# Attention logits from 64-row products, the heads in turn on the two halves of the TensorE array

## The chip, the cores and the metric

The kernel runs on one core of one Trainium2 chip. The metric is the device time of one execution in microseconds (us), the median of several runs. A second, profiled execution gives the trace from which the views below are taken; its time is given beside its span.

## The reference

One decoder layer over 2048 rows of width 1024, in fp32. What matters here are the two kinds of attention logits, both with heads of 64 channels:

```python
h = rms_norm(x, pre_norm_g[layer])
proj = h @ w_in[layer]
a_u, a_v, sq, sk, sv, mq, z = jnp.split(proj, split_at, axis=-1)
...
# window attention: 4 query heads, 2 key heads (g = 2 queries per key head), blocks of 128 rows
logits = jnp.einsum('bnqhgd,bnjhd->bnhgqj', qb, kb).astype(jnp.float32) * (dh ** -0.5)
...
# cross-attention: 4 heads into 256 memory tokens
logits = jnp.einsum('bshd,bmhd->bhsm', q, mem_k).astype(jnp.float32) * (dh ** -0.5)
...
y = jnp.concatenate([y_a, y_b, y_c], axis=-1) * jax.nn.silu(z)
x = x + rms_norm(y @ w_out[layer], post_norm_g[layer])
```

## The kernel before

Every fp32 operand of a product is held as two fp32r pieces, a rounded one (called the high piece) and the remainder (the low piece). An ordinary product takes three passes over the array: high by high, high by low, low by high. `split` makes the two pieces: a ScalarE (ACT) cast for the high one, a VectorE (DVE) subtraction for the low one.

The rows are worked on in four stretches t = 0 to 3 of 512 rows. In each, the order on TensorE is written out by hand: the v projection (line 1152), then the projections sv, k, q (two), mq (two) and z (four) in `group` (line 452), in odd stretches also the product for u and z of two stretches together (line 896, `set_a`). A last phase multiplies by w_out (line 1476). Between every six matmuls of 512 columns stands a `slot()`; tables of numbers at the head of the file say at which slot of which stretch a step is issued: loads, splits, the three stages of each attention unit (`A_STARTS`, `A_TURN`, `A_END`). TensorE and SyncE (SP, which issues the loads and stores) keep the order of the code; a scheduler orders the other engines.

An attention unit has three stages: logits and softmax, transposition of the probabilities, product with the values. A window unit (lines 622 to 680) does one block of 128 rows for all four heads, so there are 4 units in each stretch. A memory unit (lines 684 to 725) does one head for 256 rows, so there are 8 in each stretch, and the unit numbers 4 to 11 go through head 0's two halves (`cc` 0 and 1), then head 1's, and so on.

Heads have 64 channels and the array has 128 rows, and the kernel before uses that so: `split_heads` (line 601) writes one head's high piece of the queries to partitions 0 to 63 and its low piece to partitions 64 to 127, from one half of the projected rows at a time, so it takes two ACT and two DVE instructions of 64 partitions for a projection. The keys are written twice, to the upper and to the lower 64 partitions (the second time by an ACT copy, line 1202; for the memory keys line 579). One matmul of 128 rows then gives (high + low) queries by the high keys, a second the same by the low keys: two passes for each head instead of three. Each logits tile `lg` fills one PSUM bank of the pool `ps_t`, which has four; transposed probabilities, value products and others take their banks from the same pool. The transposed pieces `pT` have one buffer in SBUF.

The lines that the prediction speaks of: 641 (window logits), 691 (memory logits), 502 (a small product with 33 rows and 4 columns, `bv`), 605 and 606 (the query splits), 1202 (the second copy of the keys), 708 (transposes of the memory unit), 153 (the low piece in `split`), 250 (a weight unit loaded back from DRAM).

Of the kernel before, what the change touches and what calls it, by code (L numbers as in the profile page):

```python
# [33 lines left out]
STORE_AFTER = 6  # L34
# [3 lines left out]
TURN_SLOT = 26  # L38
# [10 lines left out]
LOADS = ((18, 25, 15, 29, 31), (66, 67, 66, 64, 68), (8, 10, 18, 19, 24, 23, 28, 31))  # L49
MAKES = ((29, 30, 30, 32, 33, 29, 42, 36),  # L50
         (70, 66, 67, 73, 76, 76, 90, 88),
         (16, 16, 21, 22, 24, 25, 34, 33))
A_STARTS = ((10, 16, 18, 26, 35, 38, 41, 41, 47, 50, 56, 58),
# [3 lines left out]
A_TURN = ((7, 10, 11, 8, 11, 8, 5, 8, 10, 9, 11, 9),  # L57
# [3 lines left out]
A_END = ((14, 14, 15, 14, 18, 10, 18, 14, 10, 13, 9, 12),  # L61
# [11 lines left out]
MIX_SLOTS = ((53, 56, 58),  # L73
             (49, 59, 61),
             (58, 61, 62),
             (62, 63, 67),
             (62, 68, 70),
             (67, 67, 73),
             (68, 72, 75),
             (73, 77, 79))  # L80
# [3 lines left out]
WO_SLOTS = ((4, 13, 13, 15, 17, 21), (35, 41, 49, 51, 58, 57))  # L84
WO_LOADS = ((-1, 3, 2, 17), (31, 29, 33, 55))
T_SLOTS = (-24, -12, -9, 4)
T_TILES = (1, 1, 1, 1)
T_STEPS = ((0, 3, 6, 6, 7), (3, 10, 10, 12, 12), (3, 5, 9, 11, 12), (2, 4, 7, 9, 9))
H_SUMS = (((-18, -14, -13, -15, -9, -7, -13, -7, -7, -6, -4),
# [7 lines left out]
H_SPARE = ((-7, 7), (20, 21))  # L97
H_LOADS = (((28, 26, 35, 39), (40, 43, 47, 42), (47, 48, 47, 54)),
           ((31, 35, 36, 32), (31, 40, 38, 41), (50, 51, 43, 57)))
H_OPS = (((35, 38, 36, 42), (52, 54, 54, 53), (49, 54, 50, 61)),  # L100
         ((37, 40, 42, 42), (50, 48, 53, 55), (52, 52, 56, 59)))
H_STORE = (3, 1)
Y_SUMS = ((-17, -11, -7), (-7, -2, -1))
Y_OPS = ((64, 71, 65, 77, 71), (71, 82, 83, 82, 82))
Y_WEIGHTS = (63, 81)
VALUES = (9, -2, 6, 6)
PUT_OFF = (5, 0, 0, 8, 6, 4)
# [3 lines left out]
def kernel(  # L111
# [227 lines left out]
    def first_stats():  # L339

        ss = tiny.tile([P, 4], F32, tag="ss", name="ss_0")
        for i in range(4):
            if i % 2 == 0:
                xp = sp.tile([P, 2, D], F32, tag="pT", name=f"xp_{i}", bufs=1)
# [72 lines left out]
    def load_x(t, ks, tag):  # L417
# [5 lines left out]
        if tag == "s4b":  # L423
            a = new_spare(1, raw=True).rearrange("p s (k n) -> p (s k) n", k=2)
        else:
            a = sp.tile([P, len(ks), TS], F32, tag=tag, name=f"xj_{t}_{ks[0]}", bufs=1)
# [46 lines left out]
    bias_0 = cp.tile([P, 4, P], F32, name="bias_0")  # L473
# [39 lines left out]
    def bias_turned():  # L513

        for i in range(2):
# [7 lines left out]
    MK = cp.tile([P, 4, 2, MEM], F32R, name="MK")  # L523
# [34 lines left out]
    def project_memory(u):  # L558
# [12 lines left out]
        if u < 2:  # L571
# [26 lines left out]
    carry = cp.tile([P, 2, 2, P], F32R, name="carry")  # L598
    SV = cp.tile([P, 5, 2, 2, 64], F32R, name="SV")

    def split_heads(ps, tag, shape_tag):
        S = sp.tile([P, 2, TS], F32R, tag=shape_tag, name=f"S_{tag}", bufs=1)
        for e in range(2):
            src = ps[64 * e : 64 * e + 64, :]
            nc.scalar.copy(S[0:64, e, :], src)  # L605
            nc.vector.tensor_tensor(S[64:128, e, :], src, f32(S[0:64, e, :]), ALU.subtract)
# [15 lines left out]
    def window_unit(t, c, S, O, done):  # L622
# [13 lines left out]
        for kv in range(2):  # L636
            hs = slice(2 * kv, 2 * kv + 2)
            lg = ps_t.tile([P, 2, 256], F32, tag="t", name=f"l_{tag}_{kv}")
            for e in range(2):
                for s in range(2):  # L640
                    nc.tensor.matmul(lg[:, e, :], S[kv][:, e, c * P : (c + 1) * P],
                                     keys[t][:, kv, s, c * P : c * P + 256], start=(s == 0), stop=(s == 1))
            if first:
                nc.vector.scalar_tensor_tensor(Lc[:, hs, :P], lg[:, :, P:], scale, bias_0[:, hs, :], ALU.mult, ALU.add)
                continue
# [11 lines left out]
        both = sp.tile([P, 2, 2, 4, P], F32R, tag="pT", name=f"pT_{tag}", bufs=1)  # L657
# [24 lines left out]
    pTs = {}  # L682

    def memory_unit(t, h, cc, S, O, done):

        tag = f"c{t}_{h}_{cc}"
        lg = ps_t.tile([P, 2, 256], F32, tag="t", name=f"l_{tag}")
        for e in range(2):
            q0 = (2 * cc + e) * P
            for s in range(2):  # L690
                nc.tensor.matmul(lg[:, e, :], S[:, h % 2, q0 : q0 + P], MK[:, h, s, :],
                                 start=(s == 0), stop=(s == 1))
# [16 lines left out]
        if cc == 0:  # L709

            pTs[h] = sp.tile([P, 2, 2, 2, 256], F32R, tag="pT", name=f"pT_{tag}", bufs=1)
# [110 lines left out]
    def first_sums():  # L822

        def some(k, s):
            r = {}

            def load():
                if k:
                    both = sp.tile([P, 2, 2, TS], F32, tag="pT", name="ya_0", bufs=1)
# [194 lines left out]
    def y_operand(src, slot, s, tag):  # L1024
# [3 lines left out]
        def load():  # L1028
            r[0] = sp.tile([P, 4, TS], F32, tag=tag, name=f"yr_{slot}", bufs=1)
# [33 lines left out]
    def attention(t, SB, SC, O, ZB):  # L1063
# [42 lines left out]
    for t in range(NT):  # L1106
# [69 lines left out]
        KK = keys[t] = sp.tile([P, 2, 2, P + TS], F32R, tag="KK", name=f"KK_{t}", bufs=1)  # L1176
        if t == 0:
            zero = sp.tile([P, 256], F32, tag="oh", name="zero", bufs=1)
            nc.vector.memset(zero, 0.0)
            for kv in range(2):  # L1180
                nc.vector.tensor_copy(KK[:, kv, :, 0:P], zero.rearrange("p (a b) -> p a b", a=2))
        else:
            nc.gpsimd.tensor_copy(KK[:, :, :, 0:P], f32(carry))
# [15 lines left out]
        for kv in range(2):  # L1199
# [430 lines left out]
```

## Time and profile before

| what | value |
|---|---|
| median of 3 runs | 750.23 us (749.23 to 751.25) |
| the profiled execution: its time | 751.22 us |
| its span, first to last instruction | 749.5 us |
| granted TensorE clock | 0.998 |
| busy: TensorE matmul, TensorE weight load | 733.6 us, 615.7 us |
| busy: DVE, ACT, POOL | 560.2 us, 477.9 us, 83.6 us |
| matmul instructions on record | 3612 |

In the views, PE is TensorE's matmul, PEld its weight load, DVE is VectorE, ACT is ScalarE, POOL is GpSimd. A row of the timeline gives start, duration from the first start to the last end, engine, line, operation, output and inputs, shapes and how many instructions; a bracket gives the idle time before it and what ended that. Matmuls are pipelined: one of 512 columns lasts about 0.39 us from start to end, and the next starts long before that end. The pace is therefore read from starts. The end of a matmul is modelled.

### The profile page before, as it was taken

To read this page: it belongs to the slowest core of one execution; us is meant where nothing else is said; L and a number is where in the kernel's file an instruction comes from. 1 tells how busy PE (TensorE), PEld (TensorE's weight loads), DVE (VectorE), ACT (ScalarE), POOL (GpSimd) and SP (SyncE) were. 2 spreads that over 40 slices of the span, in tenths; PEclk is the share of its full clock that TensorE was granted. 3 is DMA by queue.
4 is the path that set the end of the run, shared out by engine and by line. 5 is a ranking of instruction groups with operands and counts; after the bars stand their busy time and mean duration, and the time that the engine had idled before them with its cause. 6 is when DMAs were issued, how large, how long until landed. Compare 5 with 4: busy or idle time off the path is not lost.

```text
span 749.5 us, 10602 instructions
## 1 busy us (share of the span) xinstructions
PE 733.6 (98%) x3612; PEld 615.7 (82%) x3612; DVE 560.2 (75%) x997; ACT 477.9 (64%) x1042; POOL 83.6 (11%) x106
## 2 busy tenths in 40 slices
PE   9999999999999999999999999999999999999996
PEld 7888888877888888887888888888888888888884
DVE  6476897699876589734896888777579657787587
ACT  7588876774699886224776783678887244544441
POOL 1020040101120000010032010221000000010011
PEclk9999999999999999999999999999999999999999
DMA  8999877999975857899999889937377797446924
GB/s 329 333 357 358 314 305 287 382 376 316 390 246 170 283 182 252 301 363 386 370 310 368 336 300 372 327 112 262 123 259 266 262 394 288 175 173 257 348 86 196
DMA packets 79829, 215.73 MB, mean 288 GB/s; under 512 B 7531, under 2 KB 16272, under 8 KB 72080
## 3 DMA queue, kind: packets, MB, share of 16 engines
q1 hardware_dynamic: 74640, 206.08, 75.9%
q10 hardware_dynamic: 5136, 8.98, 3.2%
q8 instruction: 28, 0.46, 0.3%
q14 instruction: 25, 0.20, 0.1%
HBM read 152.11 MB, written 63.97 MB: 288 GB/s over the span
## 4 chain that ended last, share of the span: by engine, by line
PE 61%; DMA 15%; DVE 9%; ACT 4%; issue 3%; POOL 1%; SPq 0%; DVEq 0%; ACTq 0%; POOLq 0%
PE X L896 12%; PE X L1476 12%; PE Y L896 6%; PE Y_S L1476 6%; PE v L1152 4%; PE g_z L452 3%; PE Z L896 3%; PE Y L1476 3%; DMA ring<-split_d 3%; DMA xs<-in_x 2%; PE sg L855 2%; DMA wraw<-in_wst 2%; PE o_c L719 1%; PE g_mq L452 1%; PE g_q L452 1%
## 5 line engine op out<-in xcount | busy, mean ns | idle before, releaser
L452 PE MATMUL g_z<-hs,ring 128*128 128x512 f32 x360 | 87.7, 394 | 1.8 <-DMA ring<-split_d 1.8
L1152 PE MATMUL v<-ring,hs 128*128 128x512 f32 x336 | 81.2, 393 | 1.5 <-DMA ring<-split_d 1.5
L452 PEld LDWEIGHTS g_z<-hs,ring 128*128 128x128 f32 x360 | 65.8, 188 | 14.9 <-DMA ring<-split_d 2.3
L1152 PEld LDWEIGHTS v<-ring,hs 128*128 128x128 f32 x336 | 61.8, 188 | 15.3 <-DMA ring<-split_d 1.9
L896 PE MATMUL X<-hs,ring 128*128 128x512 f32 x288 | 71.0, 395 | 0.0
L896 PEld LDWEIGHTS X<-hs,ring 128*128 128x128 f32 x288 | 52.5, 188 | 10.1
L452 PE MATMUL g_mq<-hs,ring 128*128 128x512 f32 x192 | 46.5, 393 | 1.3 <-DMA ring<-split_d 1.3
L452 PE MATMUL g_q<-hs,ring 128*128 128x512 f32 x192 | 45.9, 392 | 0.0
L452 PEld LDWEIGHTS g_mq<-hs,ring 128*128 128x128 f32 x192 | 35.2, 188 | 8.5 <-ACT S_q L605 1.7
L452 PEld LDWEIGHTS g_q<-hs,ring 128*128 128x128 f32 x192 | 35.6, 188 | 7.2
L153 DVE TENSOR_TENSOR ring<-wraw_a,ring 128x1024 fp32r<-128x1024 f32 x28 | 34.6, 1235 | 6.5 <-ACT ring L152 6.2
L1349 POOL TENSOR_TENSOR r<-a,mhalf 128x1 f32<-128x1 f32 x16 | 12.8, 802 | 222.4 <-issue 140.2
L663 POOL TENSOR_SCALAR_AFFINE_SELECT pT_b<-pT_b 128x512 fp32r<-128x512 f32 x30 | 21.7, 723 | 121.9 <-ACT pT_b L152 109.7
L1476 PE MATMUL Y_S<-hs,yop 128*128 128x512 f32 x144 | 33.1, 389 | 0.0
L1476 PEld LDWEIGHTS Y_S<-hs,yop 128*128 128x128 f32 x144 | 27.0, 188 | 5.6
L619 ACT ACTIVATE L_c<-L_c,den_c 128x256 f32<-128x256 f32 x64 | 28.9, 507 | 3.3 <-DVE den_c L617 3.3
L153 DVE TENSOR_TENSOR ring<-wraw,ring 128x1024 fp32r<-128x1024 f32 (+1 forms) x18 | 21.0, 1164 | 13.1 <-ACT ring L152 12.9
L1317 ACT ACTIVATE junk<-oa 128x512 f32<-128x512 f32 x16 | 10.1, 634 | 31.9 <-DVE oa L1523 22.8
L1476 PE MATMUL X<-hs,yop 128*128 128x512 f32 x120 | 30.4, 389 | 0.0
L1476 PE MATMUL X<-hs,ring 128*128 128x512 f32 x120 | 30.4, 389 | 0.0
L152 ACT CAST ring<-wraw_a 128x1024 fp32r<-128x1024 f32 x28 | 29.4, 1049 | 1.0 <-DMA wraw_a<-in_wst 0.8
L650 ACT ACTIVATE Lc_b<-Lc_b,nm_b 128x129 f32<-128x129 f32 x64 | 25.0, 394 | 7.7 <-DVE nm_b L648 7.6
(291 smaller groups left out, 1758.3 us busy)
## 6 DMA issues: line engine op xcount, KB each, us to landing
ring<-split_d SPq DMA_DIRECT2D x38, 1024.0 KB, 7.3
split_d<-ring SPq DMA_DIRECT2D x12, 1024.0 KB, 9.1
wraw<-in_wst SPq DMA_DIRECT2D x21, 512.0 KB, 6.7
hs<-wo_B SPq DMA_DIRECT2D x8, 1024.0 KB, 11.8
y<-yd SPq DMA_DIRECT2D x8, 1024.0 KB, 10.5
xs<-in_x SPq DMA_DIRECT2D x24, 256.0 KB, 6.5
hd_S<-h SPq DMA_DIRECT2D x24, 256.0 KB, 9.4
hrS<-hd_S SPq DMA_DIRECT2D x24, 256.0 KB, 5.0
```

Of the source, the lines that this page charges most:

```text
L152: a = nc.scalar.copy(hi, src)
L153: b = (lo_engine or nc.vector).tensor_tensor(lo, src, f32(hi), ALU.subtract)
L452: nc.tensor.matmul(ps, w[:, wi, k * P : (k + 1) * P], h(t, hi, k), start=(n == 0), stop=(n == 3 * KC - 1))
L619: last = nc.scalar.mul(p[:, e, :], p[:, e, :], den[:, e : e + 1])
L650: nc.scalar.activation(Lc[:, h, : P + 1], Lc[:, h, : P + 1], AF.Exp, bias=nm[:, h : h + 1], accum_out=den[:, h : h + 1])
L663: nc.gpsimd.affine_select(prev[:, s], f32(own[:, s]), [[0, 4], [-1, P]], ALU.is_gt, 0.0, base=0, channel_multiplier=1)
L855: nc.tensor.matmul(pg[:, i, :], vg[:, i, :], wsp[:, g, :], start=True, stop=True)
L896: nc.tensor.matmul(banks[g], w[:, wi, k * P : k * P + P], at_slot(places[op], hi, k), start=first and i == 0, stop=i == 11, skip_group_che ...
L1152: nc.tensor.matmul(vps[i], h(t, hi, 2 * j + kk)[:, i * P : (i + 1) * P], w[:, wi, kk * 512 : (kk + 1) * 512], start=(j == 0 and (hi, wi, k ...
L1317: nc.scalar.activation(junk, o[:, c], AF.Square, accum_out=ss[:, col : col + 1])
L1349: nc.gpsimd.tensor_tensor(r, a, mhalf2[:, 0:1], ALU.pow)
L1476: nc.tensor.matmul(banks[m], a(s, k)[:, m * P : (m + 1) * P], w(v, k), start=first and n == 0, stop=n == 11, skip_group_check=not first)
```

## The change

1. The queries of a pair of heads are split as they come from the projection (`split_rows`): one ACT and one DVE instruction of 128 partitions, one head on partitions 0 to 63 and the other on 64 to 127. The columns of the q weights are put in another order on the way in, so that each projection holds one query head of either key head.
2. Keys are held once: `KK`, `MK` and `carry` are half as large, and the copies to the other 64 partitions are gone.
3. The logits are products over 64 rows, three for each head (high by high, low by high, high by low; the product of the two remainders is left out). The two heads of a pair take turns, one on the upper and one on the lower half of the array, each into a bank of its own.
4. Memory logits are computed for two heads at once: the unit of the even head issues the products for both and keeps the odd head's bank for the odd head's unit. The units go through both heads of a pair for `cc` 0, then for `cc` 1.
5. `pT` has two buffers; `bias_0` is a temporary tile from the `ZB` buffers instead of a lasting one.
6. The tables of slots are new. `STORE_AFTER` goes from 6 to 1; every call of `store_later` gives a number of its own, so it acts only on the count before the last flush, which stores everything in any case.

```diff
-A_STARTS = ((10, 16, 18, 26, 35, 38, 41, 41, 47, 50, 56, 58),
+A_STARTS = ((11, 16, 18, 26, 35, 38, 41, 41, 47, 56, 56, 58),
...
-    MK = cp.tile([P, 4, 2, MEM], F32R, name="MK")
+    MK = cp.tile([P, 2, 2, MEM], F32R, name="MK")
...
-            for e in range(2):
-                h = 2 * u + e
-                src = mks[64 * e : 64 * e + 64, :]
-                split(MK[0:64, h, 0, :], MK[0:64, h, 1, :], src)
-                nc.scalar.copy(MK[64:128, h], f32(MK[0:64, h]))
+            split(MK[:, u, 0, :], MK[:, u, 1, :], mks)
...
-    def split_heads(ps, tag, shape_tag):
+    def split_rows(ps, tag, shape_tag):
         S = sp.tile([P, 2, TS], F32R, tag=shape_tag, name=f"S_{tag}", bufs=1)
-        for e in range(2):
-            src = ps[64 * e : 64 * e + 64, :]
-            nc.scalar.copy(S[0:64, e, :], src)
-            nc.vector.tensor_tensor(S[64:128, e, :], src, f32(S[0:64, e, :]), ALU.subtract)
+        split(S[:, 0], S[:, 1], ps)
         return S
...
-        for kv in range(2):
+        lgs = [ps_t.tile([P, 2, 256], F32, tag="t", name=f"l_{tag}_{kv}") for kv in range(2)]
+        for e in range(2):
+            for n, (sq, sk) in enumerate(((0, 0), (1, 0), (0, 1))):
+                for kv, rows in enumerate((slice(0, 64), slice(64, P))):
+                    nc.tensor.matmul(lgs[kv][:, e, :], S[e][rows, sq, c * P : (c + 1) * P],
+                                     keys[t][rows, sk, c * P : c * P + 256], start=(n == 0), stop=(n == 2))
+        for kv, lg in enumerate(lgs):
             hs = slice(2 * kv, 2 * kv + 2)
-            lg = ps_t.tile([P, 2, 256], F32, tag="t", name=f"l_{tag}_{kv}")
-            for e in range(2):
-                for s in range(2):
-                    nc.tensor.matmul(lg[:, e, :], S[kv][:, e, c * P : (c + 1) * P],
-                                     keys[t][:, kv, s, c * P : c * P + 256], start=(s == 0), stop=(s == 1))
...
-        both = sp.tile([P, 2, 2, 4, P], F32R, tag="pT", name=f"pT_{tag}", bufs=1)
+        both = sp.tile([P, 2, 2, 4, P], F32R, tag="pT", name=f"pT_{tag}", bufs=2)
...
-        lg = ps_t.tile([P, 2, 256], F32, tag="t", name=f"l_{tag}")
-        for e in range(2):
-            q0 = (2 * cc + e) * P
-            for s in range(2):
-                nc.tensor.matmul(lg[:, e, :], S[:, h % 2, q0 : q0 + P], MK[:, h, s, :],
-                                 start=(s == 0), stop=(s == 1))
+        if h % 2 == 0:
+            lgs = [ps_t.tile([P, 2, 256], F32, tag="t", name=f"l_c{t}_{h + i}_{cc}") for i in range(2)]
+            pair_logits[h + 1] = lgs[1]
+            for e in range(2):
+                qs = slice((2 * cc + e) * P, (2 * cc + e + 1) * P)
+                for n, (sq, sk) in enumerate(((0, 0), (1, 0), (0, 1))):
+                    for lg, rows in zip(lgs, (slice(0, 64), slice(64, P))):
+                        nc.tensor.matmul(lg[:, e, :], S[rows, sq, qs], MK[rows, h // 2, sk, :], start=(n == 0), stop=(n == 2))
+        lg = lgs[0] if h % 2 == 0 else pair_logits.pop(h)
...
-            i, cc = divmod(n - 4, 2)
-            return memory_unit(t, i, cc, SC[i // 2], lambda: out_tile("C"),
+            u, cc, e = (n - 4) // 4, (n - 4) // 2 % 2, n % 2
+            return memory_unit(t, 2 * u + e, cc, SC[u], lambda: out_tile("C"),
...
-        for kv in range(2):
-            src = ps[64 * kv : 64 * kv + 64, :]
-            split(KK[0:64, kv, 0, P:], KK[0:64, kv, 1, P:], src)
-            nc.scalar.copy(KK[64:128, kv, :, P:], f32(KK[0:64, kv, :, P:]))
+        split(KK[:, 0, P:], KK[:, 1, P:], ps)
...
+    def heads(w, c0, e):
+        return np.concatenate([w[:, c0 + 128 * kv + 64 * e : c0 + 128 * kv + 64 * e + 64] for kv in range(2)], axis=1)
...
+    units += [channels(heads(w_in, 1024, e), 0) for e in range(2)]
```

TensorE, the first window unit of stretch 0 in the kernel before: `g_mq` is a projection, `svt` a transposition of values, `l_b_0_0` and `l_b_0_1` are the unit's two logits tiles, `gm` a product for the memory keys and values.

```order
L452 MATMUL g_mq_0_678<-hs_80,ring_86 128x512 x12
L1213 MATMUL svt_697<-ident,sc_sv_442 128x128 x4
L452 MATMUL g_mq_0_678<-hs_81,ring_86 128x512 x6
L641 MATMUL l_b_0_0_718<-KK_398,S_q_0_531 128x256 x4
L641 MATMUL l_b_0_1_724<-KK_398,S_q_1_627 128x256 x4
L452 MATMUL g_mq_0_678<-hs_81,ring_86 128x512 x6
L564 MATMUL gm_755<-hs_83,s4a 128x256 x24
```

The same place in the kernel after. The row pair of a dotted line comes three times for each of the two query tiles, 12 matmuls in all.

```order
L452 MATMUL g_mq_0_663<-hs_81,ring_86 128x512 x12
L633 MATMUL l_b_0_0_705<-KK_397,S_q_0_525 128x256
L633 MATMUL l_b_0_1_706<-KK_397,S_q_0_525 128x256
...
L633 MATMUL l_b_0_0_705<-KK_397,S_q_1_616 128x256
L633 MATMUL l_b_0_1_706<-KK_397,S_q_1_616 128x256
...
L564 MATMUL gm_735<-hs_83,s4a 128x256 x12
L1206 MATMUL svt_748<-ident,sc_sv_440 128x128 x4
L564 MATMUL gm_735<-hs_83,s4a 128x256 x12
```

Eight matmuls of 128 rows have become twelve of 64 rows, which go from tile to tile, and so from one half of the array to the other, at every step.

TensorE, the first memory unit at the turn from stretch 0 to stretch 1, before: `l_c_0_0` is head 0, `cc` 0, and `l_c_0_1` the same head's other rows; `v_0` to `v_3` are the v projection of the next stretch.

```order
L656 MATMUL tp_b_3_1194<-ident,Lc_b_3_1023 128x128 x4
L452 MATMUL g_z_7_1154<-hs_81,ring_85 128x512 x6
L691 MATMUL l_c_0_0_1217<-MK,S_mq_0_746 128x256 x4
L1152 MATMUL v_0_1233<-ring_86,hs_82 128x512 x6
L1152 MATMUL v_1_1234<-ring_86,hs_82 128x512 x6
L1152 MATMUL v_2_1235<-ring_86,hs_82 128x512 x6
L691 MATMUL l_c_0_1_1262<-MK,S_mq_0_746 128x256 x4
```

And after: heads 0 and 1 together, six matmuls each in turn.

```order
L650 MATMUL tp_b_3_1193<-ident,Lc_b_3_1009 128x128 x4
L452 MATMUL g_z_7_1140<-hs_81,ring_85 128x512 x6
L688 MATMUL l_c_0_0_1216<-MK,S_mq_0_697 128x256
L688 MATMUL l_c_1_0_1217<-MK,S_mq_0_697 128x256
...
L1149 MATMUL v_0_1241<-ring_86,hs_82 128x512 x6
L1149 MATMUL v_1_1242<-ring_86,hs_82 128x512 x6
L1149 MATMUL v_2_1243<-ring_86,hs_82 128x512 x6
L1149 MATMUL v_3_1244<-ring_86,hs_82 128x512 x6
```

Two bursts of four matmuls have become one of twelve, and head 1's bank is taken as early as head 0's.

ACT, stretch 1, around the keys and the first queries, before: `KK` are the keys, `S_q_0` the first query tile, `pT` transposed probabilities, `SV` the values.

```order
L1202 CAST KK_1538<-KK_1538 64x2x512
L152 CAST KK_1538<-g_k_1590 64x512
L619 ACTIVATE L_c_3_1_1645<-L_c_3_1_1645,den_c_3_1_1647 128x256 x2
L152 CAST SV<-svt_1702 128x8x64
L1202 CAST KK_1538<-KK_1538 64x2x512
L605 CAST S_q_0_1715<-g_q_0_1676 64x512
L722 COPY oh_c_2_1_1725<-o_c_2_1_1720 64x512
L605 CAST S_q_0_1715<-g_q_0_1676 64x512
```

After:

```order
L152 CAST KK_1526<-g_k_1581 128x512
L612 ACTIVATE L_c_3_1_1648<-L_c_3_1_1648,den_c_3_1_1650 128x256 x2
L152 CAST s4a<-h_0_0_1383 128x512
L719 COPY oh_c_0_1_1674<-o_c_0_1_1669 64x512
L152 CAST pT_c_3_0_1707<-tp_c_3_0_1702 128x2x256
L152 CAST S_q_0_1716<-g_q_0_1678 128x512
L152 CAST SV<-svt_1721 128x8x64
```

One cast of 128 partitions stands for the keys where four instructions stood, and one for the query tile where two stood.

More of the change, by code (lines that the diff above doesn't have):

```diff
@@ L72 @@
 SEQ_A = tuple((op, g) for op in FIRST_OPS for g in range(4)) + LAST_SEQ
[L73 to L78, printed above, removed]
+MIX_SLOTS = ((52, 52, 56),
+             (48, 59, 61),
+             (58, 59, 61),
+             (57, 60, 64),
+             (63, 68, 70),
+             (61, 66, 72),
              (68, 72, 75),
-             (73, 77, 79))
+             (75, 77, 79))
 W_ORDER = ("B11", "T1", "B22", "T3", "T2")
@@ L83 @@
 COPY_SLOT = 45
-WO_SLOTS = ((4, 13, 13, 15, 17, 21), (35, 41, 49, 51, 58, 57))
-WO_LOADS = ((-1, 3, 2, 17), (31, 29, 33, 55))
-T_SLOTS = (-24, -12, -9, 4)
+WO_SLOTS = ((5, 13, 13, 16, 17, 21), (34, 40, 46, 50, 57, 61))
+WO_LOADS = ((-2, 3, 3, 18), (29, 30, 33, 56))
+T_SLOTS = (-24, -11, -9, 7)
 T_TILES = (1, 1, 1, 1)
-T_STEPS = ((0, 3, 6, 6, 7), (3, 10, 10, 12, 12), (3, 5, 9, 11, 12), (2, 4, 7, 9, 9))
-H_SUMS = (((-18, -14, -13, -15, -9, -7, -13, -7, -7, -6, -4),
[7 rows of a table removed]
[L97 to L107, printed above, removed]
+T_STEPS = ((0, 3, 6, 6, 7), (0, 8, 9, 11, 11), (0, 7, 9, 9, 12), (0, 3, 5, 9, 9))
+H_SUMS = (((-20, -15, -14, -14, -10, -8, -14, -8, -8, -7, -5),
[7 rows of a table added]
+H_SPARE = ((-10, 2), (21, 24))
+H_LOADS = (((25, 28, 36, 40), (40, 41, 42, 42), (47, 49, 47, 53)),
+           ((29, 35, 39, 30), (35, 43, 44, 44), (50, 50, 43, 56)))
+H_OPS = (((36, 37, 37, 43), (51, 54, 53, 51), (49, 52, 50, 61)),
+         ((37, 40, 42, 42), (47, 47, 52, 55), (58, 52, 55, 57)))
+H_STORE = (4, 2)
+Y_SUMS = ((-20, -19, -11), (-5, -4, 0))
+Y_OPS = ((64, 70, 64, 79, 69), (69, 76, 78, 80, 80))
+Y_WEIGHTS = (66, 81)
+VALUES = (12, -1, 8, 7)
+PUT_OFF = (5, 0, 0, 8, 8, 4)
 @with_exitstack
@@ L343, in first_stats @@
             if i % 2 == 0:
-                xp = sp.tile([P, 2, D], F32, tag="pT", name=f"xp_{i}", bufs=1)
+                xp = sp.tile([P, 2, D], F32, tag="pT", name=f"xp_{i}", bufs=2)
             xs = xp[:, i % 2, :]
@@ L425, in load_x @@
         else:
-            a = sp.tile([P, len(ks), TS], F32, tag=tag, name=f"xj_{t}_{ks[0]}", bufs=1)
+            a = sp.tile([P, len(ks), TS], F32, tag=tag, name=f"xj_{t}_{ks[0]}", bufs=2 if tag == "pT" else 1)
         step = ks[1] - ks[0]
@@ L513, in bias_turned @@
     def bias_turned():
+        bias_0 = late["bias_0"] = sp.tile([P, 4, P], F32, tag="ZB", name="bias_0", bufs=2)
         for i in range(2):
@@ L709, in memory_unit @@
         if cc == 0:
-            pTs[h] = sp.tile([P, 2, 2, 2, 256], F32R, tag="pT", name=f"pT_{tag}", bufs=1)
+            pTs[h] = sp.tile([P, 2, 2, 2, 256], F32R, tag="pT", name=f"pT_{tag}", bufs=2)
         pT = pTs[h]
@@ L828, in load @@
                 if k:
-                    both = sp.tile([P, 2, 2, TS], F32, tag="pT", name="ya_0", bufs=1)
+                    both = sp.tile([P, 2, 2, TS], F32, tag="pT", name="ya_0", bufs=2)
                     r["11"], r["21"] = both[:, 0], both[:, 1]
@@ L1028, in load @@
         def load():
-            r[0] = sp.tile([P, 4, TS], F32, tag=tag, name=f"yr_{slot}", bufs=1)
+            r[0] = sp.tile([P, 4, TS], F32, tag=tag, name=f"yr_{slot}", bufs=2 if tag == "pT" else 1)
             nc.sync.dma_start(r[0], src.rearrange("k p n -> p k n"))
@@ L1173 @@
         moments[t] = scale_and_shift(st, t)
-        KK = keys[t] = sp.tile([P, 2, 2, P + TS], F32R, tag="KK", name=f"KK_{t}", bufs=1)
+        KK = keys[t] = sp.tile([P, 2, P + TS], F32R, tag="KK", name=f"KK_{t}", bufs=1)
         if t == 0:
@@ L1179 @@
             nc.vector.memset(zero, 0.0)
[L1180 to L1181 removed]
+            nc.vector.tensor_copy(KK[:, :, 0:P], zero.rearrange("p (a b) -> p a b", a=2))
         else:
[L1183 removed]
+            nc.gpsimd.tensor_copy(KK[:, :, 0:P], f32(carry))
             nc.gpsimd.tensor_copy(SV[:, 0], f32(SV[:, 4]))
@@ L1198 @@
         ps = group(weight_unit(U_K, t), t, f"k{t}", ps_t)
-        for kv in range(2):
-            src = ps[64 * kv : 64 * kv + 64, :]
-            split(KK[0:64, kv, 0, P:], KK[0:64, kv, 1, P:], src)
-            nc.scalar.copy(KK[64:128, kv, :, P:], f32(KK[0:64, kv, :, P:]))
+        split(KK[:, 0, P:], KK[:, 1, P:], ps)
         if t < NT - 1:
-            nc.gpsimd.tensor_copy(carry, f32(KK[:, :, :, TS:]))
+            nc.gpsimd.tensor_copy(carry, f32(KK[:, :, TS:]))
         slot()
@@ L1595 @@
     units = [row_pairs(w_in, 512, j) for j in range(4)]
-    units += [channels(w_in, c) for c in (1408, 1280, 1024, 1152, 1536, 1664)]
+    def heads(w, c0, e):
+        return np.concatenate([w[:, c0 + 128 * kv + 64 * e : c0 + 128 * kv + 64 * e + 64] for kv in range(2)], axis=1)
+    units += [channels(w_in, c) for c in (1408, 1280)]
+    units += [channels(heads(w_in, 1024, e), 0) for e in range(2)]
+    units += [channels(w_in, c) for c in (1536, 1664)]
     units += [channels(w_in, 1792 + P * i) for i in range(8)]
```

35 lines of the change are left out of this document (17 added, 18 removed), and 32 rows, old and new, of tables (A_END, A_STARTS, A_TURN, H_SUMS).

## The prediction

> **What bounds the kernel now.** I read the page's first part, then the waits of PE, then busy time by stretch. The busy times and shares of the engines, and every wait of PE (in all, how often, the longest):
>
> ```profile
> PE 733.6 (98%) x3612; PEld 615.7 (82%) x3612; DVE 560.2 (75%) x997; ACT 477.9 (64%) x1042; POOL 83.6 (11%) x106
> PE g_z L452 <- DMA ring<-split_d: 1.8, 1, 1.8
> PE warm L334 <- POOL ident masks.py:199: 1.8, 1, 1.8
> PE tp_c L708 <- DVE pT_c L153: 1.7, 1, 1.7
> PE v L1152 <- DMA ring<-split_d: 1.5, 2, 1.3
> PE g_mq L452 <- DMA ring<-split_d: 1.3, 1, 1.3
> PE o_b L673 <- POOL pT_b L665: 0.5, 1, 0.5
> ```
>
> PE is busy for 98% of the span and waits 8.6 us in all. The waits say nothing of PE being held up inside its own stream, so the stretches matter too (busy us of PE, PEld, DVE, ACT, POOL):
>
> ```profile
> 112.00:306.00 194.00, 190.51 (x972) 160.81 (x971) 155.60 (x291) 142.66 (x325) 18.81 (x23) 1.00 0.81 287
> 390.00:590.00 200.00, 198.05 (x1017) 167.53 (x1016) 155.63 (x282) 143.51 (x325) 20.94 (x25) 1.00 0.77 275
> ```
>
> In the two long stretches that hold most of the attention PE is idle for 3.49 and 1.95 us, while DVE and ACT have 38 to 57 us of room in each. So a microsecond added to PE's own stream is a microsecond of the time; one taken from DVE or ACT counts only where PE waits for it. Of the 8.6 us, 1.8 (before the warm-up matmuls) is untouched by the change, and 6.8 can go at most.
>
> **The logits before.** The pace of matmuls of 512 columns from the chain's longest piece; then a window burst and a memory burst with what follows each; then how many there are.
>
> ```profile
> 589.80 21.76 PE X L1476 x96
> 64.69 1.12 PE L641 MATMUL l_b<-KK,S_q 128*128 128x256 f32 x8
> 65.65 1.55 PE L452 MATMUL g_mq<-hs,ring 128*128 128x512 f32 x6
> 129.49 0.63 PE L691 MATMUL l_c<-MK,S_mq 128*128 128x256 f32 x4
> 129.96 1.56 PE L1152 MATMUL v<-ring,hs 128*128 128x512 f32 x6
> L691 PE MATMUL l_c<-MK,S_mq 128*128 128x256 f32 x128 | 20.6, 286 | 0.0
> L641 PE MATMUL l_b<-KK,S_q 128*128 128x256 f32 x128 | 18.2, 285 | 0.0
> ```
>
> 21.76 / 96 gives 0.227 us for 512 columns. From start to the next line's start a window unit takes 65.65 - 64.69 = 0.96 us, 0.12 for each of 8 matmuls; a memory unit 0.47 us, two of them 0.94. The 256 matmuls make 16 window units and 32 memory units, and after the change 16 window units and 16 pairs: 32 bursts of twelve in place of about 0.95 us each.
>
> **The new bursts, and what a seam costs.** If the two halves of the array run side by side, two matmuls take the time of one, and twelve take 6 x 0.12 = 0.72 us, which is 0.24 less than a window unit took. But no row shows two halves at work, and one thing stands against the gain: one product in the kernel does not use the whole array, `bv`, with 33 rows and 4 columns. Here are its neighbours on PE and on PEld, with the durations of the kinds:
>
> ```profile
> 10.64 0.84 PE L1152 MATMUL v<-ring,hs 128*128 128x512 f32 x3
> 11.41 0.80 PE L502 MATMUL bv<-hot_t,rel_t 33*4 33x383 f32 x2
> 12.14 0.73 PE L1152 MATMUL v<-ring,hs 128*128 128x512 f32 x2
> 10.87 0.19 PEld L1152 LDWEIGHTS v<-ring,hs 128*128 128x128 f32 x1
> 11.41 0.09 PEld L502 LDWEIGHTS bv<-hot_t,rel_t 33*4 33x4 f32 x2 [0.35 <-issue]
> 12.14 0.53 PEld L1152 LDWEIGHTS v<-ring,hs 128*128 128x128 f32 x3 [0.65 <-issue]
> L502 PE MATMUL bv<-hot_t,rel_t x2: 482/482/482, 11.4 to 11.7; 33*4 33x383 f32 x2
> L1152 PE MATMUL v<-ring,hs 128*128 128x512 f32 x336 | 81.2, 393 | 1.5 <-DMA ring<-split_d 1.5
> ```
>
> Everywhere else a weight load starts as the matmul before it starts, and is hidden. Here the loads wait. The third v starts at 10.64 + 0.84 - 0.39 = 11.09, and bv's load only at 11.41, 0.32 later where 0.227 is the pace: 0.09 lost. The two passes of bv are 0.80 - 0.48 = 0.32 apart, so they need 0.64 of the 0.73 until the next v: 0.09 lost again. That v's weights are then loaded in the open: the second v comes 0.73 - 0.39 = 0.34 after it, 0.11 over the pace. In all 0.29 us. bv's own weights have 4 columns; weights of 128 columns on the way in add the same 0.11. So I put a burst's two seams at 0.40 us, with 0 as the other end, should the loss belong to the narrow columns and not to the rows.
>
> The Trainium skill, in "TensorEngine Tiling (Array Packing)", Key Properties, says that going from one tiling mode to another drains TensorE, and that changing the tile within a mode does not. By that rule every new burst pays both seams; the trace agrees, with 0.09 us on either side of bv.
>
> The sum for a burst: 0.72 + 0.40 = 1.12 us, 0.16 more than a window unit's 0.96 and 0.18 more than two memory units' 0.94; with 16 of each, 16 x 0.16 + 16 x 0.18, **+5.4 us**. The ends: with no seams 0.72 against 0.96, 32 x 0.24 = 7.7 us less; with the halves one after the other 12 x 0.12 + 0.40 = 1.84, 32 x 0.88 = 28.2 us more.
>
> Whether the halves overlap, the same skill in "TensorE: Matmul & The Clock Gate", Part 3, gives a rule: matmuls on different row groups run together, each further tile about 4 ns later, and a weight load passes a running matmul only where their row groups differ. By it the six pairs would last about 0.75 us (an estimate from that page's 4 ns), which changes the sum by 0.8 us. Its second half is not what this trace shows: whole-array loads hide behind whole-array matmuls, PE and PEld being busy for 733.6 + 615.7 us of a span of 749.5.
>
> **The splits and the copies.** ACT and DVE for queries and keys, and an ACT cast of 128 partitions to compare:
>
> ```profile
> L605 ACT CAST S_mq<-g_mq 64x512 fp32r<-64x512 f32 x16 | 9.3, 583 | 10.6 <-PE g_mq L452 7.1 <-DVE S_mq L606 2.5 <-DMA wo<-in_wst 0.8
> L605 ACT CAST S_q<-g_q 64x512 fp32r<-64x512 f32 x16 | 9.3, 581 | 13.2 <-DVE S_q L606 7.1 <-PE g_q L452 6.0
> L606 DVE TENSOR_TENSOR S_mq<-g_mq,S_mq 64x512 fp32r<-64x512 f32 x16 | 11.0, 689 | 1.3 <-ACT S_mq L605 0.9
> L606 DVE TENSOR_TENSOR S_q<-g_q,S_q 64x512 fp32r<-64x512 f32 x16 | 11.0, 689 | 6.9 <-ACT S_q L605 6.7
> L1202 ACT CAST KK<-KK 64x1024 fp32r<-64x1024 f32 x8 | 8.3, 1045 | 1.3 <-DVE KK L153 1.0
> L152 ACT CAST pT_b<-tp_b 128x512 fp32r<-128x512 f32 x16 | 9.4, 585 | 5.7 <-PE tp_b L656 3.4 <-PE o_b L673 2.2
> ```
>
> An instruction over 128 partitions takes as long (585 ns) as one over 64 (583), so half of the 32 query splits go: 9.3 us of ACT, 11.0 of DVE; the second copies of the keys take another 8.3 of ACT, and the halved splits of the keys a few more on both. Nearly all of this lies beside PE's work. What it can reach is the one wait of PE for DVE, 1.7 us (tp_c for the low piece of pT), which the second pT buffer eases as well. I take 1.7 for it, and of the 4.6 us of waits for reloaded weights 0.8: the new slots move loads and stores on SP's queue to other places, and nothing before the run says which of these waits stay, so I allow from all 6.8 gone to as much again added. Together **-2.5 us**. Smaller copies on POOL (11% busy) and one copy less at the start cost and bring nothing; the temporary `bias_0` holds one ZB buffer until the first window unit, beside PE work that has its inputs.
>
> **Sum.** +5.4 - 2.5 = +2.9 us. The profiled execution took 751.22 us, 1.72 beyond its span and 1.0 above the median of the runs, so the same sum is 754.1 there, and 750.2 + 2.9 = **753.1 us** as a median. About 0.3%, 2.25 us, is what a measurement of this kernel can tell from no change; the forecast is just past it.
>
> **Rivals.**
>
> *The seams are cheap* (ends on the other side). If the 0.29 us at bv come from its 4 columns, and 64 rows with all 128 columns need no draining, a burst takes 0.72 us: -7.7 - 2.5, so 740.0 us. For it: bv differs in rows and columns at once, and the trace cannot part them. Against: the load of bv's weights itself waited, before any narrow column had worked. It decides where both seams cost less than 0.24 us a burst; below that the bursts alone are a gain.
>
> *The halves do not run side by side*, so the change does not do what it says: weights come one after the other, at the 0.12 us that a matmul of 256 columns needs now. With seams +28.2 - 2.5, 776 us; without them 32 x 0.48 = 15.4, 763 us. For it: in all rows above a weight load starts only with the matmul before it, one at a time. Against: there is one set of rows in all of them, so none had to be loaded for the other half.
>
> *Banks.* A pair takes two of the four banks at once, and the odd head's stays taken until its unit's slot, in stretch 0 up to 9 slots later (47 to 56 in A_STARTS), 9 x 6 x 0.227 = 12 us. A transposition or value product without a bank stops PE, and all that is queued behind it, until ACT has read the odd head's logits. If four of the 16 pairs meet a wait like the longest of PE's, 1.8 us, that is 7 us on top of the forecast: 760. Against it: no wait of PE for a logits bank stands in the list.
>
> **How the numbers follow.** Forecast 0.42, cheap seams 0.28, no overlap 0.20 (0.12 with seams), banks 0.10. The forecast lies by the bound of the same, and its own range is 749 to 758 by the waits: of its 0.42, 0.03 is faster, 0.15 the same, 0.24 slower. Cheap seams are faster but for 0.01; no overlap is slower; of the banks 0.01 is the same. That gives faster 0.30, same 0.17, slower 0.53. The range from 738 to 764 takes in cheap seams, the forecast, the banks and no overlap without seams; 776 and the edges are left out, some 0.16.
>
> **What would show it.** Right: starts of the two halves a few ns apart in each pair; about 0.1 us between the last whole-array matmul's end of streaming and the first 64-row load, and the same after; a burst of 1.1 us; PE's waits near 6 us. Cheap seams: 0.7 to 0.8 us from a burst's first start to the next line's, with its load hidden. No overlap: starts 0.12 apart within a pair. Banks: waits of PE at tp or o for ACT's exponentials. If the bursts take 0.96 us or less, the sum fails at the seams; if they take 1.1 and the time still falls, it fails at the waits.

## The result and the profile after

| what | before | changed |
|---|---|---|
| median, runs on one chip | 749.73 us (747.30 to 751.25, 6 runs) | 753.29 us (752.85 to 754.07, 6 runs) |
| the profiled execution | 751.22 us, span 749.5 us | 752.85 us, span 751.1 us |

The ratio is 1.0051, with a 95% interval of 1.0033 to 1.0070: the changed kernel is slower by about 3.6 us. Two later repeats of the changed kernel (run to have it beside experiments) gave 1.0045 (1.0026 to 1.0064) and 1.0046 (1.0027 to 1.0064). The two profiled executions differ by only 1.6 us, because the one of before is at the top of its kernel's runs. This gap between a profile and a median matters below. Beside the experiments the kernel before ran 70 more times, on four chips; one of these runs, 813.66 us at a granted clock of 0.849, is in a slower state of the chip and is left out. The spans of the other 69 have a median of 747.2 us. The 25 among them with a granted clock of 0.998, the clock of the profiled execution, spanned 744.5 to 748.7 us, 745.6 in the median; the profiled execution spanned 749.5.

The busy times of the engines in the changed kernel, from the page:

```profile
PE 739.0 (98%) x3740; PEld 608.6 (81%) x3740; DVE 545.4 (73%) x974; ACT 452.0 (60%) x1008; POOL 82.6 (11%) x106
```

The change did what it says for the lighter engines: ACT is busy for 25.9 us less and DVE for 14.8 us less than before. TensorE is busy for 5.4 us more, and the time went with TensorE. The waits of PE in the changed kernel (in all, how often, the longest):

```profile
PE warm L334 <- POOL ident masks.py:199: 1.8, 1, 1.8
PE o_c L716 <- ACT L_c L698: 1.2, 1, 1.2
PE g_mq L452 <- DMA ring<-split_d: 0.9, 1, 0.9
PE tp_c L705 <- DVE OC L721: 0.3, 1, 0.3
PE l_c L688 <- DVE OB L672: 0.2, 1, 0.2
PE g_k L452 <- DMA ring<-split_d: 0.2, 1, 0.2
PE g_z L452 <- DMA ring<-split_d: 0.2, 1, 0.2
```

They are 4.8 us in all, where they were 8.6. The wait of tp_c for the low piece of pT is gone, and the waits for reloaded weights fell from 4.6 to 1.3 us. One wait is new: a value product that needs ACT to have read logits, 1.2 us, the kind that the prediction listed under banks. The same two stretches as before, busy us of PE, PEld, DVE, ACT, POOL:

```profile
112.00:306.00 194.00, 192.22 (x1011) 157.47 (x1010) 151.93 (x287) 135.22 (x315) 19.43 (x23) 1.00 0.81 286
390.00:590.00 200.00, 200.00 (x1067) 165.48 (x1066) 153.99 (x278) 137.50 (x319) 21.76 (x26) 1.00 0.77 267
```

In the second stretch PE is busy for all of the 200 us. Less work on ACT and DVE can't shorten such a stretch.

The first window burst and its neighbours, on PE and on the weight loads (start, duration from the first start to the last end, then the work):

```profile
61.69 4.01 PE L452 MATMUL g_mq<-hs,ring 128*128 128x512 f32 x17
65.64 0.97 PE L633 MATMUL l_b<-KK,S_q 64*128 64x256 f32 x12
66.54 0.74 PE L564 MATMUL gm<-hs,s4a 128*128 128x256 f32 x4
65.64 0.77 PEld L633 LDWEIGHTS l_b<-KK,S_q 64*128 64x128 f32 x12 [0.35 <-issue]
```

Read this against the rows of before. There a window unit's first start stood 0.96 us before the next line's; here it is 66.54 - 65.64 = 0.90 us, for twelve matmuls in place of eight. But the burst now also waits at its edges: the weight load starts only with the burst, after 0.35 us without a load. The single starts of this burst show it all, in ns from the burst's first start:

```
last g_mq         -319          227 is the pace: 92 lost
first pair           0     3
second pair        223   226    117 is the pace: about 106 lost to the open load
pairs 3 to 6       340   343,   458   461,   575   578,   693   696
first gm           900          204 after the last start: about 89 lost
second gm         1124          120 is the pace: about 104 lost to the open load
```

The two halves of a pair start 3 ns apart, and from the second on pairs follow each other in 117 to 118 ns. In the list, the open load is the time for which the products stand until their weights are in, because no load could run ahead. The first two products last 381 ns where the later ones last 274 to 278, which is that time again. Added up, the seams are 92 + 106 + 89 + 104 = 391 ns. The median over the 32 bursts is 0.901 us from the first start to the next line's, and with the 0.092 ahead and the 0.104 behind a burst costs 1.10 us.

### The profile page after: what moved, and what is told of

The parts are those of the page before. It is cut to its first block, busy times and chain, and to the rows that moved or that the text cites. A ratio compares the mean times of both kernels' runs of the same rounds, so it can differ in the third digit from the quotient of the medians.

```text
span 751.1 us, 10789 instructions
## 1 busy us (share of the span) xinstructions
PE 739.0 (98%) x3740; PEld 608.6 (81%) x3740; DVE 545.4 (73%) x974; ACT 452.0 (60%) x1008; POOL 82.6 (11%) x106
## 4 chain that ended last, share of the span: by engine, by line
PE 72%; DMA 13%; DVE 8%; ACT 4%; SPq 1%; issue 1%; POOL 0%; DVEq 0%; ACTq 0%; POOLq 0%
PE X L1469 12%; PE g_z L452 10%; PE X L893 9%; PE v L1149 6%; PE Y_S L1469 6%; PE g_mq L452 5%; PE g_q L452 4%; PE Y L893 3%; PE Y L1469 3%; DMA ring<-split_d 3%; PE gm L564 2%; PE l_b L633 2%; DMA h<-hraw 2%; DMA yd<-c 2%; PE o_b L667 2%; PE g_k L452 1%
## 5 line engine op out<-in xcount | busy, mean ns | idle before, releaser
L452 PE MATMUL g_z<-hs,ring 128*128 128x512 f32 x360 | 89.7, 398 | 0.2 <-DMA ring<-split_d 0.2
L893 PE MATMUL X<-hs,ring 128*128 128x512 f32 x288 | 71.5, 396 | 0.0
L698 ACT ACTIVATE L_c<-l_c,nm_c 128x256 f32<-128x256 f32 x48 | 22.3, 475 | 15.6 <-DVE nm_c L693 15.5
L871 ACT ACTIVATE vg<-vg,vsum,vrstd 128x128 f32<-128x128 f32 x64 | 26.5, 487 | 7.9 <-DMA vg<-vhat_d 7.9
L984 DVE TENSOR_TENSOR h<-h,h 128x512 f32<-128x512 f32 x32 | 23.1, 721 | 10.9 <-DMA h<-hraw 10.6
```

The source lines that it names most:

```text
L452: nc.tensor.matmul(ps, w[:, wi, k * P : (k + 1) * P], h(t, hi, k), start=(n == 0), stop=(n == 3 * KC - 1))
L698: nc.scalar.activation(p[:, e, :], lg[:, e, :], AF.Exp, bias=nm[:, e : e + 1], scale=scale, accum_out=den[:, e : e + 1])
L871: nc.scalar.activation(vg[t, g][:, i, :], vg[t, g][:, i, :], AF.Identity, bias=nb[:, c], scale=rv[:, c])
L893: nc.tensor.matmul(banks[g], w[:, wi, k * P : k * P + P], at_slot(places[op], hi, k), start=first and i == 0, stop=i == 11, skip_group_che ...
L984: nc.vector.tensor_tensor(r[into, k], r[x, k], r[y, k], op)
```

## The experiments

The theory: a burst of 64-row products costs two seams of 0.20 us each, the halves run side by side, and the two nearly cancel. The rivals: seams are cheap and the time is lost elsewhere; the halves do not overlap; banks; and the new slots.

**Whole-array bursts.** The twelve products are replaced by eight of 128 rows at the same places, and everything else stays as changed. The logits are then summed over the pair of heads, and the low pieces of the queries are not read.

```diff
-            for n, (sq, sk) in enumerate(((0, 0), (1, 0), (0, 1))):
-                for kv, rows in enumerate((slice(0, 64), slice(64, P))):
-                    nc.tensor.matmul(lgs[kv][:, e, :], S[e][rows, sq, c * P : (c + 1) * P],
...
+            for kv in range(2):
+                for s in range(2):
+                    nc.tensor.matmul(lgs[kv][:, e, :], S[e][:, 0, c * P : (c + 1) * P],
+                                     keys[t][:, s, c * P : c * P + 256], start=(s == 0), stop=(s == 1))
```

> The changed kernel with its slots, splits and buffers, but each burst of twelve 64-row products is replaced by eight 128-row products (the logits come out as sums over a pair of heads, with two passes of the high queries by the high and the low keys: this part of the computation is changed). Seams theory (a burst of the changed kernel takes 1.10 us by its trace, of which 0.40 is entering and leaving the 64-row mode, and the slots and lighter engines gain 1 to 2.5 us): the burst goes back to 0.95, 32 x 0.15 = 4.8 us less than the changed kernel's 753.3, so 748.5, a little under the kernel before. Rival (seams cheap, the new slots lose the time): bursts go from 0.72 to 0.95, 7.4 us more, 760.7.

It took 750.09 us (748.46 to 753.42, 12 runs), 1.0016 of the kernel before (0.9999 to 1.0033), and its profiled span was 747.2 us. A second set, run later:

> The kernel with whole-array bursts in place of the 64-row ones (logits summed over the pair), again: 750 us as in its first run, 2.5 to 3.5 us less than the changed kernel, and no difference from the kernel before beyond 0.3%.

This gave 750.23 us and 1.0023 (1.0002 to 1.0045), with a span of 748.9. The rows of the first set, again at the first window unit:

```profile
62.80 2.66 PE L452 MATMUL g_mq<-hs,ring 128*128 128x512 f32 x11
65.30 1.11 PE L633 MATMUL l_b<-KK,S_q 128*128 128x256 f32 x8
66.25 1.60 PE L564 MATMUL gm<-hs,s4a 128*128 128x256 f32 x12
```

The burst lasts 66.25 - 65.30 = 0.95 us, with no seam: its first start is 65.30 - (62.80 + 2.66 - 0.39) = 0.23 us after the last g_mq, which is the pace. Two things follow. The 64-row form is what makes the changed kernel slower than this one, by 2.1 to 3.2 us in the medians. And beside whole-array bursts the rest of the change (splits, keys, pT, slots) brings nothing: this kernel has it all, and is at best level with the kernel before. It has one thing easier, as no burst of it waits for the low pieces of the queries; but no wait of a burst for a split stands in the changed kernel's list above either.

PE waits longer in this kernel than in the changed one, 6.0 us in all in the first set's profile and 6.2 in the second's, where the changed kernel has 4.8. Two waits that the changed kernel's list doesn't have:

```profile
PE o_c L716 <- DVE pT_c L153: 1.7, 1, 1.7
PE l_c L688 <- ACT svs L1190: 1.0, 1, 1.0
```

**One more whole-array product, ahead of the burst or in its middle.** Both kernels do the same extra work, one product of 256 columns per burst, which the next product to that tile overwrites. In the middle it parts the burst, so that there are four seams.

```diff
         for e in range(2):
+            if e == 0:
+                nc.tensor.matmul(lgs[0][:, e, :], S[e][:, 0, c * P : (c + 1) * P],
+                                 keys[t][:, 0, c * P : c * P + 256], start=True, stop=True)
```

In the second kernel the condition is `e == 1`.

> The changed kernel with one more whole-array product of 256 columns just ahead of each burst, into a bank that the burst then overwrites (results unchanged). Both theories: 32 x 0.12 = 3.8 us more than the changed kernel, 757.1. It is the base for the next kernel.

> The same extra whole-array product, but in the middle of each burst, between the products of the first and of the second query tile, so that each burst has four seams in place of two. Seams theory: 32 x 0.40 = 12.8 us more than with the product ahead, 769.9. Rival (seams cheap): the same as with the product ahead, 757.1.

Ahead: 756.54 us (755.91 to 758.10), ratio 1.0097 (1.0069 to 1.0125). In the middle: 766.87 us (766.35 to 767.27), ratio 1.0229 (1.0197 to 1.0261). The second kernel's first window unit:

```profile
65.42 0.62 PE L636 MATMUL l_b<-KK,S_q 64*128 64x256 f32 x6
65.97 0.39 PE L632 MATMUL l_b<-KK,S_q 128*128 128x256 f32 x1
66.28 0.62 PE L636 MATMUL l_b<-KK,S_q 64*128 64x256 f32 x6
66.83 1.34 PE L564 MATMUL gm<-hs,s4a 128*128 128x256 f32 x9
```

The burst is now 1.41 us long. The same extra product costs 3.2 to 4.2 us where it stands ahead, beside whole-array work, and 10.3 us more in the middle: 10.3 / 32 = 0.32 us for each further pair of seams (0.39 by the burst's length in the trace). Below 0.24 us for a burst's two seams the bursts alone would have been a gain, as the prediction said. Cheap seams are refuted.

**One half only.** Both heads of a pair are computed on the upper half, so the second head's logits are a copy of the first's. The work and the seams stay, the overlap goes.

```diff
-                for kv, rows in enumerate((slice(0, 64), slice(64, P))):
+                for kv, rows in enumerate((slice(0, 64), slice(0, 64))):
```

> The changed kernel with both heads of a pair on the upper half of the array, twelve products in the same order (the second head's logits are those of the first: this part of the computation is changed). Overlap theory: 12 steps of 0.116 us in place of 6, 32 x 0.70 = 22.3 us more, 775.6. If the halves did not run side by side in the changed kernel: no change, 753.3.

It took 773.66 us (771.94 to 774.72), ratio 1.0330 (1.0306 to 1.0354). The first window unit:

```profile
65.34 1.68 PE L633 MATMUL l_b<-KK,S_q 64*128 64x256 f32 x12
66.95 1.33 PE L564 MATMUL gm<-hs,s4a 128*128 128x256 f32 x9
```

The burst takes 1.61 us in place of 0.90, twelve steps of 0.12 in place of six. The two halves do run side by side in the changed kernel, and that is worth 20 to 21 us.

**The order of the products.** Two kernels keep the twelve products and both halves, and issue them three upper and three lower in turn, or six upper and then six lower.

```diff
-            for n, (sq, sk) in enumerate(((0, 0), (1, 0), (0, 1))):
-                for kv, rows in enumerate((slice(0, 64), slice(64, P))):
+            for kv, rows in enumerate((slice(0, 64), slice(64, P))):
+                for n, (sq, sk) in enumerate(((0, 0), (1, 0), (0, 1))):
```

> The changed kernel with the twelve products of a burst in another order: three on the upper half, then three on the lower, for each query tile (results unchanged). Overlap theory: only the products on either side of a change of half overlap, 9 steps in place of 6, 32 x 3 x 0.116 = 11.1 us more, 764.4. Rival (the halves' starts 3 ns apart are only how the records are written, the work is done one after the other): no change, 753.3.

> The changed kernel with all six products of the upper half first and then all six of the lower half (results unchanged). After the run with three and three, which cost nothing: if each half has a queue of its own and a matmul of one half may start ahead of earlier ones of the other, 753 to 755, and the second half's first start within 0.1 us of the first half's. If three and three was only hidden by a short look ahead: up to 11 steps in place of 6, 32 x 5 x 0.116 = 18.6 us more, 771.9.

Three and three: 752.44 us (751.59 to 754.37), ratio 1.0040 (1.0022 to 1.0057), no slower than the changed kernel. My expectation of 764.4 fell. Six and six: 762.17 us (761.51 to 762.46), ratio 1.0177 (1.0156 to 1.0198), between the two expected values. The starts within the first window burst, in ns:

```
three and three   0 10   223 233   340 350   458 468   575 585   693 703
six and six       0   223   340 347   458   569 575   688 693   805   923   1042
one half only     0   223   340   458   575   693   812   933   1050   1167   1287   1407
```

With three and three the starts come in pairs, 10 ns apart, much as they do when the halves alternate. With six and six there are two rows of starts. The first is 0, 223, 340, 458, 575, 693: the same six numbers with which the kernel on one half alone begins. The second is 347, 569, 688, 805, 923, 1042, and it too begins with a step of 222 ns, the open load. So the lower half's first product, the seventh in the program, starts 7 ns after the third and 111 ns ahead of the fourth. With three and three the fourth product starts ahead of the second and the third.

The records don't name the half, so which start belongs to which is inferred. But in the kernel on one half alone no two products of a burst start within 110 ns of each other, so starts 7 or 10 ns apart belong to different halves; and as three or six products of one half come first in the program, one of the two starts ahead of products issued before it. Measured is that the overlap is complete at a distance of three products. At six the burst is 1.25 us long, between 0.90 and 1.61, so half of the overlap is lost.

**The slots of before.** All the tables of numbers of the kernel before, in the changed kernel.

```diff
-A_STARTS = ((11, 16, 18, 26, 35, 38, 41, 41, 47, 56, 56, 58),
+A_STARTS = ((10, 16, 18, 26, 35, 38, 41, 41, 47, 50, 56, 58),
```

> The changed kernel with every table of slots of the kernel before (64-row products, single keys, pairs of memory heads and two pT buffers stay). Seams theory: the bursts' 32 x 0.15 = 4.8 us stay; if the new slots were worth 1 to 2 us in waits, those come back: 753 to 756. Rival (the new slots lose the time, the products do not): back to the kernel before, 749.7.

It took 772.74 us (772.15 to 774.20), ratio 1.0323 (1.0300 to 1.0345). Both expectations missed. Its longest waits of PE, beside the 1.8 us before the warm-up matmuls:

```profile
PE o_c L716 <- ACT pT_c L152: 6.1, 2, 3.7
PE v L1149 <- DMA ring<-split_d: 1.9, 1, 1.9
PE g_k L452 <- DVE OC L721: 1.7, 1, 1.7
PE o_c L716 <- ACT L_c L698: 1.6, 1, 1.6
PE l_c L688 <- DVE pT_c L153: 1.6, 1, 1.6
```

In all PE waits 18.0 us, 12.7 more than in the changed kernel that ran beside it. PE is also busy for 745.0 us, 5.8 more for the same products, at a granted clock of 0.991 in place of 0.997. The old numbers belong to another order of the heads: unit 5 was head 0's second half and is now head 1's first, whose bank is taken a unit early. That this is what the waits come from is likely and not shown. What is shown is that the changed kernel needs new slots; whether these would bring anything to the kernel before was not run.

**The splits in two halves.** The changed kernel, with two instructions of 64 partitions on each engine for a query split, as before the change.

```diff
-        split(S[:, 0], S[:, 1], ps)
+        for r in (slice(0, 64), slice(64, P)):
+            split(S[r, 0], S[r, 1], ps[r, :])
```

> The changed kernel with each query split in two instructions of 64 partitions on ACT and two on DVE, as before the change (some 9 us more work on ACT and 11 on DVE, the same results). If lighter ACT and DVE brought part of the 2.5 us that the prediction took for the waits, this gives a part of it back, 754 to 755.5 us, with longer waits of PE for the splits or the transposed probabilities. Rival: the splits lie beside PE's work entirely, and it takes 752.5 to 753.3 us as the changed kernel does, with PE's waits near 5 us.

It took 759.68 us (758.26 to 760.58), ratio 1.0136 (1.0111 to 1.0161); the changed kernel beside it took 752.31. The cost of 7.4 us is more than either theory gave. Most of it is at one place, 452 us into the span, where a window burst stops in the middle (a bracket is the wait before the row's first product, and what ended it):

```profile
452.32 0.73 PE L634 MATMUL l_b<-KK,S_q 64*128 64x256 f32 x7
453.67 0.38 PE L634 MATMUL l_b<-KK,S_q 64*128 64x256 f32 x2 [0.61 <-ACT S_q L152]
456.58 0.79 PE L634 MATMUL l_b<-KK,S_q 64*128 64x256 f32 x3 [2.53 <-DVE S_q L153]
457.30 5.08 PE L452 MATMUL g_mq<-hs,ring 128*128 128x512 f32 x12
```

And the busy us and the granted clock in the second wait and just after it (the last three columns are the clock, the DMA share and GB/s):

```profile
453.00:454.90 1.90, 0.43 (x3) 0.19 (x2) 1.07 (x2) 0.59 (x2) 0.00 (x0) 1.00 1.09 433
455.00:457.00 2.00, 0.42 (x3) 0.42 (x3) 1.50 (x3) 0.00 (x0) 0.00 (x0) 0.50 0.99 267
457.00:461.60 4.60, 4.60 (x13) 3.50 (x12) 4.10 (x8) 1.43 (x7) 0.00 (x0) 0.50 0.85 342
```

The burst waits 0.61 + 2.53 us for the second query tile's pieces. Within the second wait, at 454.9 us, the granted clock falls to 0.50, and by the trace's record of the clock it stays there for 6.8 us: the twelve g_mq take 5.08 us where 11 x 0.227 + 0.39 = 2.89 is usual. That is 3.1 + 2.2 = 5.3 us, nearly all of the 5.5 us by which this profile's span, 758.1, is longer than the 752.6 of the changed kernel beside it. So the lighter splits are not worthless in the changed kernel; at this place its slots are set as close as the lighter splits allow, and rely on them.

**Bursts joined.** If a seam costs 0.2 us, fewer and longer bursts should help. The fourth window unit of each stretch goes to the slot of the first memory unit, with its later stages kept near their old slots.

```diff
-A_STARTS = ((11, 16, 18, 26, 35, 38, 41, 41, 47, 56, 56, 58),
+A_STARTS = ((11, 16, 18, 35, 35, 38, 41, 41, 47, 56, 56, 58),
...
-A_TURN = ((9, 10, 11, 8, 8, 6, 6, 6, 11, 6, 10, 8),
+A_TURN = ((9, 10, 11, 4, 8, 6, 6, 6, 11, 6, 10, 8),
```

> The changed kernel with the fourth window unit of each stretch moved to the slot of the first memory unit, so that their two bursts stand one behind the other: 28 excursions into 64-row products in place of 32. By the seams, 0.40 us each, 4 x 0.40 = 1.6 us less, 751 us. Rival: the two bursts take all four banks, and a transposition or value product behind them waits until the exponentials have read one; one wait of 2 us in each stretch would be 8 us more, 761 us, with waits of PE at tp or o for ACT or DVE.

It took 785.54 us (779.15 to 787.27), ratio 1.0475 (1.0431 to 1.0518). The longest waits of PE:

```profile
PE tp_b L650 <- ACT Lc_b L612: 9.0, 3, 5.1
PE l_c L688 <- DVE OB L672: 6.8, 3, 3.9
PE l_c L688 <- DVE pT_b L153: 2.4, 1, 2.4
```

And the joined bursts of stretch 0:

```profile
107.25 0.97 PE L633 MATMUL l_b<-KK,S_q 64*128 64x256 f32 x12
108.06 0.28 PE L688 MATMUL l_c<-MK,S_mq 64*128 64x256 f32 x1
110.88 1.62 PE L688 MATMUL l_c<-MK,S_mq 64*128 64x256 f32 x11 [2.55 <-DVE OB L672]
```

The first product of the second burst starts; the other head's has no bank until DVE has read an earlier unit's output, 2.5 us later. Those are 9.2 us of waits for banks. The 9.0 us of tp_b are of another kind: the moved unit has only 4 slots between its logits and its transposition, which its exponentials and normalisation overrun. In all PE waits 25.2 us. The rest goes with the clock, 0.980 against 0.997: PE is busy for 750.8 us, 11.8 more than in the changed kernel for the same products. The saved seams, 1.6 us, don't show. No kernel of the study beats the kernel before.

**The changed kernel again**, as a measure beside the others, twice:

> The changed kernel as it is, timed again beside the next kernel on the same chip: both theories 753.3 us, 0.5% over the kernel before.

> The changed kernel on the same chip as the kernel with split halves, as its measure: 752.5 to 753.3 us.

752.45 us (751.14 to 753.57, 8 runs) and 752.31 us (750.49 to 754.32, 12 runs), with spans of 751.8 and 752.6.

## Why the prediction was right, and where it was not

The forecast was 753.1 us and the result 753.29. Its sum was +2.9 us, the measured difference +3.6. Point by point:

- *What bounds the kernel* (PE's own stream): held. ACT and DVE have 40.7 us less work, and the time is longer.
- *The halves side by side*: held. Starts are 3 ns apart in each pair; without the overlap the time is 20 to 21 us more.
- *A burst's seams at 0.40 us, from the neighbours of bv*: held. They are 0.39 us in the trace of the changed kernel, and 0.32 to 0.39 from the pair of kernels with the extra product. All four pieces are there, two drains of 0.09 and two open loads of 0.10 to 0.11. The rule that the prediction named from the Trainium skill, "TensorEngine Tiling (Array Packing)", Key Properties, that changing the tiling mode drains TensorE, agrees: 0.09 us on either side.
- *The bursts' term, +5.4 us*: right in sign and mechanism, too large. A burst took 1.10 us, not 1.12, so that the trace gives 32 x (1.10 - 0.95) = +4.8. Place by place, from the start ahead of each burst to the second start behind it, a burst costs 0.147 us more than in the kernel with whole-array bursts (the median of the 32), which makes +4.7. In time, against the same kernel with whole-array bursts, it is +2.1 to +3.2 by the medians, and +3.8 by the spans (the mean of 751.1, 751.8 and 752.6 against that of 747.2 and 748.9). The waits account for the spans: PE waits 4.8, 5.3 and 5.5 us in the three profiles of the changed kernel and 6.0 and 6.2 in the two with whole-array bursts, 0.9 less in the mean, and 4.7 - 0.9 = 3.8. So the slower stream hides waits that the faster one meets. Two of the three profiles of the changed kernel were the longest run of their set, so the spans say rather too much, and the medians are the better measure of the time.
- *The waits' term, -2.5 us*: this step failed. The waits on the page did fall, by 3.8 us. But the kernel with all of the change except the 64-row bursts is no faster than the kernel before, at 1.0016 (0.9999 to 1.0033) and 1.0023 (1.0002 to 1.0045): +1.2 and +1.7 us. With the bursts in, the difference of 3.4 to 3.6 us less the trace's 4.7 for the bursts leaves a gain of 1.1 to 1.3 us, half of the term. The step read the waits of one execution as those of every execution. That one spanned 749.5 us, about 4 us more than the median of the 25 other runs of the kernel before at the same granted clock, and more than any of them. As the products are the same in all of them, part of its 8.6 us of waits was most likely its own; the other runs left no trace that would show it.
- The bursts' term was put too high and the waits' term promised more than came, so the two errors have opposite signs and the sum came out nearer than its terms. The base helped too: it was 750.23 us in the three runs known then and 749.73 in six. That the forecast lies within 0.2 us of the result is luck; that the time rises is not, as the bursts' term held in sign and mechanism.
- *The splits at nothing beside PE's work*: right for taking work away, wrong as a rule. Giving the same work back with the new slots costs 7.4 us. The prediction saw that this work lies beside PE's, and not how little room is left between its end and PE's need of it.
- *Banks*: one wait of 1.2 us, not four of 1.8. The joined bursts show the mechanism at its full price, 9.2 us of waits for four moved units.

What stays open: the kernel before with the new slots alone, and the doubled keys with the new slots, were not run, so the worth of each smaller edit is known only as a sum.

## What to carry to other kernels

On a kernel that TensorE bounds, price an excursion into 64-row products as a fixed cost (two drains, two open weight loads) against what the paired products save. Here, with products of 256 columns, the cost is 0.4 us and six pairs for eight whole-array products save 0.24 us, so an excursion pays only where it saves more than three matmuls' time, at 0.12 us each. Longer bursts spread the seams but hold more banks, and banks that come late can cost more than the seams, here 9.2 us against 1.6. A table of slots that is tuned to a load can carry no slack: before work is given back to an engine that looks idle, look at what is queued behind it. And before a wait on a page is counted as something to win, ask whether the profiled execution is a usual one: compare its span with those of other runs at the same granted clock.

## What the hardware showed unexpectedly

- Products of one half of the array can run beside products of the other half that are not next to them in the program, and start ahead of products that were issued before them. At a distance of three the overlap was complete (752.4 us); at six, half of it was gone (762.2 us), and the seventh product started with the third, ahead of the fourth. The Trainium skill, "TensorE: Matmul & The Clock Gate", Part 3, says that matmuls start and end strictly in program order; the starts at 0 and 10 ns with three and three in turn, and the two rows of starts with six and six, do not fit that.
- A stall was paid twice. PE stood for 0.61 and 2.53 us with two products between them, and in the second wait the granted clock fell to 0.50 for 6.8 us, which cost another 2.2 us. In the kernels with the old slots and with joined bursts, which wait more, the clock is at 0.50 three and six times before the span's end, each time for 3.4 or 6.8 us, in or just behind idle stretches of PE of 1.6 to 5.1 us; others of 1.6 and 1.9 us brought none.
